# Two transformer mixers: the delta rule's solve is traced ahead of the attention heads, and its products are regrouped

## The chip, the cores and the metric

One core of one Trainium2 chip runs the whole program. The metric is the device time of one execution in microseconds (us). A core has a matrix engine (TensorE: PE in the profile, its weight loads PEld), a vector engine (VectorE, DVE), a scalar engine (ScalarE, ACT), GpSimd (POOL) and a queue engine (SyncE, SP). Each runs its own list of instructions in order; semaphores and DMA landings hold an instruction back until its data are there. TensorE writes its results to PSUM, eight banks of 512 f32 columns per partition, from which VectorE and ScalarE read.

## The reference

The program is two blocks in f32 on 256 tokens of width 1024. The change lies in the second block, whose two layers (l = 0, 1) each hold one mixer and one feed-forward part (dense in layer 0, a mixture of experts in layer 1). The mixer runs two branches on the same normed input h and adds them, gated:

```python
proj = h @ w_in[l]                    # q, k, v of the delta rule; z, b, a; the attention's q, k, v, gates; m_g
qkv = causal_conv_silu(dn_qkv, conv_w[l]);  d_q, d_k, d_v = split(qkv)      # 8 heads of 64
d_q = l2_norm(d_q) * 64 ** -0.5;  d_k = l2_norm(d_k)
o_a = gated_delta_rule(d_q, d_k, d_v, sigmoid(dn_b), g_log)
y_a = (rms_norm(o_a, dn_norm[l]) * silu(dn_z)) @ w_oa[l]
o_b = nsa_core(...)                   # compressed, selected and windowed attention, 8 heads
y_b = o_b @ w_ob[l]
y = (gate_a * y_a + gate_b * y_b) @ w_out[l]
x = x + g_m * y
```

In the delta rule each token t subtracts what earlier tokens left in the state, so the new values X solve a unit lower triangular system per head: (I + L) X = V, with L[t, s] = beta[t] * (k_t . k_s) * exp(g_t - g_s) for s < t. The output is A X, where A holds the same products with q in place of k, kept for s <= t.

## The kernel before

Instructions are traced into a tile framework. Its planner simulates the five engines and, at each moment, gives an engine the ready instruction that was traced first; so the order of the source lines is an order of rank, and work of a lower rank fills the gaps of work of a higher one. What comes out is one fixed list per engine. A tile name with `bufs=n` owns n buffers; a further tile of that name waits until one is released. PSUM is shared as three banks for the linear layers (`pl`), two for the delta rule (`pm`) and three for the attention (`pn`).

Linear layers (`lin_fm`, L263; `lin_tm`, L277) load weights by SP, split each into a high part (`wh`, ScalarE) and a low part (`wl`, VectorE), and multiply in three products (`mm3`, L256). `lin_fm` takes 256 output columns at a time: 48 matmuls for 1024 inputs.

`mixer` (L824) traces in this order: the token-major columns 2048 to 3367 (`lin_tm`, L864, into `tm`); the attention's preparation (`nsa`, L865: compression, norms, rotary embedding, up to `nqT`, `nkT`, `npcT`); q and k of the delta rule with convolution and SiLU (`lin_fm ... conv`, L866, into `dq`); the attention heads (`heads()`, L867: scores, softmax, transposes, into `obh`, `obl`); `delta` (L868); v and z (L869, L870); the rest of the delta rule (`solve()`, L871, into `dz`); then the gates (L886, L887, into `mg`), `w_ob` on the heads' output (`branch_b`, reads `obh`), the split of the solve's output into `oah`, `oal`, and `w_oa` (`branch_a`, reads `oah`). In layer 0 the modulation products (`ada`, tiles `adaw`) fill as well. `w_out` and the feed-forward part read what `branch_a` makes.

`delta` (L900) norms q and k (L905), computes decays, then loops over eight heads (L942): five products into one `pm` bank and an exponential (`ddd`), the key products `p0` (keys of the first 128 tokens against q and k of all 256, 512 columns, L957) and `p_1` (keys of the last 128 against the last 128, 256 columns, L958), each over 64 partitions, two VectorE products into `dUA` (A0, UA1), and the diagonal 16 by 16 blocks, which GpSimd's queue scatters to `dUb`. A 15-step substitution on VectorE inverts these (`dtp`, `dWb`), a round trip through DRAM lays them out (`ds`, `dc16`), and `inv32` widens them to 32 by 32 (`dtf`).

`solve` (L1018) goes through eight row blocks n of 32 tokens, T, cc = n // 4, n % 4. A block subtracts from V the products of L with the X of all blocks before (matmuls `pm<-dX,dUA`), writes `dRt` (VectorE), multiplies by the inverse (`pm<-dRt,dtf`) and copies X out of PSUM (ScalarE, `dX`), each in two halves of four heads. For the second tile (T = 1) every block takes one product with all 128 rows of the first tile's X and, from cc = 1, one with the second tile's:

```python
lst.append((A0(h)[:, 1, 128 + 32 * cc:160 + 32 * cc], X[:, 0, xc]))
if cc:
    lst.append((UA1[0:32 * cc, h, 1, r], X[0:32 * cc, 1, xc]))
```

After blocks 3 and 7 the outputs of a tile are made (`dUA,dX`), normed (`dsq`) and multiplied into `dz`. An f32 product is two matmul instructions in the trace.

Of the kernel before, what the change touches and what calls it, by code (L numbers as in the profile page):

```python
# [26 lines left out]
F32 = mybir.dt.float32  # L27
# [4 lines left out]
AF = mybir.ActivationFunctionType  # L32
OP = mybir.AluOpType
AX = mybir.AxisListType.X
# [55 lines left out]
class Net:  # L90
# [733 lines left out]
    def mixer(self, l):  # L824
        nc, tc, a = self.nc, self.tc, self.a
        with ExitStack() as cx:
            p1 = cx.enter_context(tc.tile_pool(name="m1_%d" % l, bufs=1))
            p2 = cx.enter_context(tc.tile_pool(name="m2_%d" % l, bufs=2))
            p0 = self.p0 = cx.enter_context(tc.tile_pool(name="m0_%d" % l, bufs=1))
            self.tags = dict(rms1=("dsq", 1))  # L830
            ring = p1.tile([128, 4, 2, 256], F32, name="ln", tag="big")
            self.ring = dict(lnt=[ring[:, i] for i in range(2)], lnsq=[ring[:, i] for i in range(2, 4)])
            cw = self.par[l][1]
            mod, scm = self.prep_mod(l, 0, 2, 0)
            hi, lo, X = self.hilo()
            if l == 0:
                self.ada()
                pss = self.nbank()[:, :256]
                add = self.square_sum(p2, pss, True)
                self.apply_ln(p2, 1, then=lambda f, x: add(x))  # L840
                self.rms_stats(pss)
            self.apply_rms(p2, scm, mod[:, 0:8], hi, lo)
            w = a["w_in_2"][l]


            dq = p0.tile([128, 8, 256], F32, name="dq")
            dv = p1.tile([128, 4, 256], F32, name="dv")

            def conv(m0, ps):
                for i in range(2):  # L850
                    m = m0 + i
                    y = p2.tile([128, 256], F32, name="cvy")
                    self.act(y, ps[:, i, :], scale=cw[:, 36 + m:37 + m])
                    for j in range(3):
                        d = 3 - j
                        self.stt(y[:, d:], ps[:, i, :256 - d], cw[:, j * 12 + m:j * 12 + m + 1], y[:, d:],
                                 OP.mult, OP.add)
                    o = dq[:, m, :] if m < 8 else dv[:, m - 8, :]
                    self.sig(o, y)
                    self.tt(o, o, y, OP.mult)  # L860
            tm = p1.tile([128, 2, 1320], F32, name="tm")
            z = p0.tile([128, 4, 256], F32, name="dz")
            self.ring = {}
            self.lin_tm(X, w, 2048, 1320, 8, lambda c, n, T, ps: self.act(tm[:, T, c:c + n], ps), step=440)  # L864
            ob, heads = self.nsa(l, p1, p2, tm)  # L865
            self.lin_fm(X, w, 0, 1024, 8, conv)  # L866
            heads()  # L867
            solve = self.delta(l, p1, p2, dq, dv, tm, z)  # L868
            self.lin_fm(X, w, 1024, 512, 8, lambda m, ps: conv(m + 8, ps))  # L869
            self.lin_fm(X, w, 1536, 512, 8, lambda m, ps: self.silu_ps(z[:, m:m + 2, :], ps))  # L870
            oa = solve()  # L871
            if l == 0:
                self.ada(2)
            mg = [p0.tile([128, 8, 256], F32, name="mg%d" % i, tag=("dq", "mg")[i]) for i in range(2)]

            def gate(i):
                self.lin_fm(X, w, 3368 + i * 1024, 1024, 8, lambda m, ps: self.sig(mg[i][:, m:m + 2, :], ps))

            def branch_b(m, ps):
                g = mg[1][:, m:m + 2, :]  # L880
                self.tt(g, g, ps, OP.mult)

            def branch_a(m, ps):
                g = mg[0][:, m:m + 2, :]
                self.tt(g, g, ps, OP.mult)
                (self.tt if m == 6 else self.ptt)(g, g, mg[1][:, m:m + 2, :], OP.add)  # L886
                self.split(yh[:, m:m + 2, :], yl[:, m:m + 2, :], g)  # L887
            gate(1)
            gate(0)
            if l == 0:  # L890
                self.ada()
            self.lin_fm(ob, a["w_ob_2"][l], 0, 1024, 4, branch_b)
            oah = p0.tile([128, 4, 256], F32R, name="oah", tag="nqT")
            oal = p0.tile([128, 4, 256], F32R, name="oal", tag="nkT")
            self.split(oah, oal, oa)
            yh, yl, Y = self.hilo()
            self.lin_fm(lambda k: (oah[:, k, :], oal[:, k, :]), a["w_oa_2"][l], 0, 1024, 4, branch_a)
        return Y

    def delta(self, l, p1, p2, dq, dv, tm, z):  # L900

        nc, tc, a = self.nc, self.tc, self.a
        c = self.c

        for m in range(0, 8, 2):  # L905
            sq = p2.tile([128, 2, 256], F32, name="dsq", bufs=1)
            self.act(sq, dq[:, m:m + 2, :], AF.Square)
            ps = self.pm.tile([128, 2, 256], F32, name="pm")
# [30 lines left out]
        le = c["le1"][:, :128]  # L939
        A0 = lambda h: UA0[h // 4][:, h % 4]  # L940
        U = lambda h, T: A0(h)[:, 1, 0:128] if T == 0 else UA1[:, h, 1, :]
        for h in range(8):  # L942
            hp, r = h // 2, slice(64 * (h % 2), 64 * (h % 2) + 64)
            gt = p2.tile([128, 2, 128], F32, name="dgt")
            for T in range(2):
                self.ts(gt[:, T, :], c["gt"], g[:, T, h:h + 1], None, OP.mult)
            pe = self.pm.tile([128, 4, 128], F32, name="pm")
            self.mm(pe[:, 0:2, :], gt[:, 0, :], c["le1"].rearrange("p (a b) -> p a b", a=2), True, False, **f)
            self.mm(pe[:, 1, :], g[:, 1, h:h + 1].to_broadcast([128, 128]), le, False, False, **f)
            self.mm(pe[:, 2, :], gt[:, 1, :], le, False, False, **f)  # L950
            self.mm(pe[:, 0, :], self.identb, self.negst, False, False, **f)
            self.mm(pe[:, 2, :], self.identb, self.negst, False, True, **f)
            dd = p2.tile([128, 3, 128], F32, name="ddd")
            self.act(dd, pe[:, 0:3, :], AF.Exp)
            p0 = self.pm.tile([128, 2, 256], F32, name="pm")
            p_1 = self.pm.tile([128, 2, 128], F32, name="pm")
            k = dq[r, 4 + hp, :]  # L957
            self.mm(p0, k[:, 0:128], dq[r, hp::4, :])  # L958
            self.mm(p_1, k[:, 128:256], dq[r, hp::4, 128:256])
            d0 = dd[:, 0:2, :].rearrange("p a b -> p (a b)")  # L960
            self.stt(A0(h), p0, be[:, 0, h:h + 1], d0[:, None, :].to_broadcast([128, 2, 256]), OP.mult, OP.mult)
            self.stt(UA1[:, h], p_1, be[:, 1, h:h + 1], dd[:, 2:3, :].to_broadcast([128, 2, 128]), OP.mult, OP.mult)

            bd = p1.tile([128, 2, 8, 16], F32, name="dbd")
            for T in range(2):
                self.tt(bd[:, T], U(h, T).rearrange("p (b j) -> p b j", j=16), b16, OP.mult)
            nc.vector.tensor_reduce(out=cb[:, :, h], in_=bd.rearrange("p t b j -> p t j b"), op=OP.add, axis=AX)
            for T in range(2):
                q = 64 * T + 8 * h
                nc.gpsimd.dma_start(out=Ub[q:q + 8].rearrange("p s j -> p (s j)"), in_=cb[:, T, h, :])  # L970

        W = p1.tile([128, 2, 16, 16], F32, name="dWb")
        tp = p1.tile([128, 16, 16], F32, name="dtp", tag="dbd")
# [44 lines left out]
    def solve(self, p1, p2, dv, z, A0, UA1, W32, dn, b64, inv32):  # L1018
# [11 lines left out]
        for n in range(8):  # L1030
# [7 lines left out]
                pq = ps[:, :256], ps[:, 256:]  # L1038
            for q in range(2):
                cq = slice(q * 256, q * 256 + 256)  # L1040
                src = V[:, 0, :]
                if n:
                    for h in range(4 * q, 4 * q + 4):
                        xc = slice(h * 64, h * 64 + 64)
                        lst = []
                        if T == 0:
                            lst.append((A0(h)[0:32 * cc, 1, r], X[0:32 * cc, 0, xc]))
                        else:
                            lst.append((A0(h)[:, 1, 128 + 32 * cc:160 + 32 * cc], X[:, 0, xc]))
                            if cc:  # L1050
                                lst.append((UA1[0:32 * cc, h, 1, r], X[0:32 * cc, 1, xc]))
                        for i, (lh, rh) in enumerate(lst):
                            self.mm(pq[q][r, (h % 4) * 64:(h % 4) * 64 + 64], lh, rh, i == 0, i == len(lst) - 1)
                    self.tt(Rt[r, cq], V[r, T, cq], pq[q][r, :], OP.subtract)
                    src = Rt
                for h in range(4 * q, 4 * q + 4):
                    xc = slice(h * 64, h * 64 + 64)
                    self.mm(pq[q][r, (h % 4) * 64:(h % 4) * 64 + 64], W32[r, T * 8 + h, :], src[r, xc])
                self.act(X[r, T, cq], pq[q][r, :])
            if n == 0:  # L1060
                inv32(1)
            if cc == 3:

                sl = slice(T * 128, T * 128 + 128)
# [831 lines left out]
```

## Time and profile before

| what | us |
|---|---|
| median of three runs | 2441.9 (2436.46 to 2446.41) |
| the profiled execution, whole | 2432.33 |
| its span, first to last instruction | 2430.5 |
| PE busy in the span | 2298.8 (95%) |
| DVE busy | 1570.5 (65%) |
| ACT busy | 1282.6 (53%) |
| first mixer: lin_tm's first copy to branch_a's end | about 547 to 828 |
| second mixer: first matmul to branch_a's end | 1114.76 to 1398 |

A busy PE is not a PE at its peak: a matmul of 256 columns lasts 0.28 us in the rows, but the next one starts 0.12 us after it. What PE gets done is read from the starts. PEclk is the granted share of TensorE's clock: 1.00 is 2.4 GHz, 0.5 is 1.2 GHz, and a value between is a stretch with both.

### The profile page before, as it was taken

The numbers are of one execution on the slowest core, as the hardware profiler recorded it, in microseconds if no ns is written. First come the engines' busy times: TensorE is split into PE (matmuls) and PEld (weight loads), VectorE is DVE, ScalarE is ACT, GpSimd is POOL, SyncE is SP. The second block draws the span as 40 slices with busy tenths as digits, with TensorE's granted clock in tenths as the row PEclk, the third lists the DMA queues.
The fourth block names the chain that finished last, engine by engine and source line by source line (L and its number), as shares of the span: only waits on it lengthen the run. The fifth ranks groups of instructions, "written<-read, shape, count | busy, mean of one in ns | idle before, by whom it ended". The sixth has DMA issues, their size and how long they took to land. (4 is left out here: it accounts for less than half of the span.)

```text
span 2430.5 us, 40562 instructions
## 1 busy us (share of the span) xinstructions
PE 2298.8 (95%) x15959; PEld 1870.7 (77%) x15959; DVE 1570.5 (65%) x2353; ACT 1282.6 (53%) x1944; POOL 389.0 (16%) x358
## 2 busy tenths in 40 slices
PE   7999999989999999998999999999999999999987
PEld 7878898878768899997878788888788888644333
DVE  5854777757864576776876469998878888511011
ACT  4654675546645344445756257778777867410010
POOL 2201311220110100000110022322331233000000
PEclk9999999999999999999999899999999999999999
DMA  6454445555354568884323358889898999999998
GB/s 201 142 146 139 159 140 172 169 186 161 115 161 139 169 224 290 282 287 141 120 72 103 133 204 317 335 306 368 315 329 330 348 334 332 370 377 408 408 408 318
DMA packets 275192, 586.92 MB, mean 241 GB/s; under 512 B 30752, under 2 KB 171296, under 8 KB 262704
## 3 DMA queue, kind: packets, MB, share of 16 engines
q1 hardware_dynamic: 260688, 577.28, 66.4%
q0 software_dynamic: 5504, 5.91, 1.4%
q8 instruction: 127, 2.08, 0.4%
q10 hardware_dynamic: 8800, 1.05, 0.3%
q14 instruction: 73, 0.60, 0.1%
HBM read 582.26 MB, written 1.64 MB: 240 GB/s over the span
## 5 line engine op out<-in xcount | busy, mean ns | idle before, releaser
L152 DVE TENSOR_TENSOR wl<-wr,wh 128x1024 fp32r<-128x1024 f32 (+3 forms) x733 | 892.4, 1249 | 307.2 <-ACT wh L149 301.4
L149 ACT ACTIVATE wh<-wr 128x1024 fp32r<-128x1024 f32 (+3 forms) x792 | 773.4, 1006 | 410.7 <-PE pl L172 207.6
L172 PE MATMUL pl<-xTh,wh 128*128 128x256 f32 x1696 | 482.8, 285 | 11.9 <-ACT wh L149 4.9
L172 PE MATMUL pl<-xTh,wl 128*128 128x256 f32 x1696 | 478.9, 284 | 0.9 <-DVE wl L152 0.8
L172 PE MATMUL pl<-xTl,wh 128*128 128x256 f32 x1696 | 478.7, 283 | 0.4 <-DVE xTl L158 0.4
L172 PE MATMUL pl<-wh,eg 128*128 128x448 f32 x1280 | 372.6, 368 | 2.3 <-ACT es L149 2.3
L172 PEld LDWEIGHTS pl<-xTh,wh 128*128 128x128 f32 x1696 | 320.1, 189 | 24.6 <-issue 9.9
L172 PEld LDWEIGHTS pl<-xTl,wh 128*128 128x128 f32 x1696 | 320.3, 189 | 7.8 <-issue 5.7
L172 PEld LDWEIGHTS pl<-xTh,wl 128*128 128x128 f32 x1696 | 319.5, 189 | 8.7 <-issue 6.4
L155 POOL TENSOR_TENSOR wl<-wr,wh 128x896 fp32r<-128x896 f32 (+1 forms) x59 | 189.7, 3216 | 490.4 <-ACT wh L149 386.7
L172 PEld LDWEIGHTS pl<-wh,eg 128*128 128x128 f32 x1280 | 241.7, 189 | 25.1 <-ACT es L149 3.4
L172 PE MATMUL pl<-wl,eg 128*128 128x448 f32 x640 | 238.0, 372 | 14.2 <-POOL wl L155 11.3
L172 PE MATMUL pl<-wr,egf 128*64 128x448 f32 x768 | 163.2, 550 | 5.3 <-DMA wr<-in_w_moe_dram 4.9
L172 PEld LDWEIGHTS pl<-wl,eg 128*128 128x128 f32 x640 | 121.1, 189 | 32.7 <-POOL wl L155 15.1
L172 PEld LDWEIGHTS pl<-wr,egf 128*64 128x64 f32 x768 | 56.2, 137 | 90.0 <-issue 68.6
L172 PE MATMUL pn<-wl,eah 128*128 128x512 f32 x280 | 112.8, 403 | 5.6 <-DVE wl L152 4.1
L172 PE MATMUL pn<-wh,eal 128*128 128x512 f32 x280 | 110.5, 395 | 0.0
L168 DVE TENSOR_SCALAR esu<-pl 128x448 f32<-128x448 f32 x24 | 20.3, 919 | 126.4 <-PE pl L172 126.4
L149 ACT ACTIVATE ehf<-pm 128x448 f32<-128x448 f32 x12 | 6.5, 543 | 165.4 <-PE pn L172 148.6
L172 PE MATMUL pn<-wr,ehf 128*64 128x512 f32 x336 | 86.4, 598 | 5.1 <-DMA wr<-in_w_moe_dram 3.9
L172 PE MATMUL pn<-wh,eah 128*128 128x512 f32 x280 | 89.9, 394 | 0.0
L149 ACT ACTIVATE es<-pl 128x448 f32<-128x448 f32 x64 | 56.9, 989 | 59.6 <-PE pl L172 59.3
(626 smaller groups left out, 3711.8 us busy)
## 6 DMA issues: line engine op xcount, KB each, us to landing
wr<-in_w_moe_dram SPq DMA_DIRECT2D x256, 896.0 KB, 7.1
wr<-in_w_moe_dram SPq DMA_DIRECT2D x96, 1024.0 KB, 8.4
wr<-in_w_dense_dram SPq DMA_DIRECT2D x42, 1024.0 KB, 7.1
wr<-in_w_in_dram SPq DMA_DIRECT2D x32, 1024.0 KB, 5.1
wr<-in_w_in_c_dram SPq DMA_DIRECT2D x30, 1024.0 KB, 5.2
adaw<-in_w_ada_dram SPq DMA_DIRECT2D x48, 512.0 KB, 4.6
adar<-in_w_ada_dram SPq DMA_DIRECT2D x48, 512.0 KB, 5.6
wr<-in_w_in_ab_dram SPq DMA_DIRECT2D x16, 1024.0 KB, 5.2
```

Of the source, the lines that this page charges most:

```text
L149: return self.nc.scalar.activation(out, in_, f, **k)
L152: return self.nc.vector.tensor_tensor(out=out, in0=a, in1=b, op=op)
L155: return self.nc.gpsimd.tensor_tensor(out=out, in0=a, in1=b, op=op)
L168: return self.nc.vector.tensor_scalar(out, a, s1, None, op0=op0)
L172: return self.nc.tensor.matmul(out=out, lhsT=l, rhs=r, start=start, stop=stop, **k)
```

## The change

In `mixer` two calls move: the q and k columns of the delta rule go ahead of `lin_tm`, and `heads()` goes behind `solve()`. In `delta` the loop over eight heads becomes a loop over four pairs: the decays of both heads first, then the two `p0` products back to back (partitions 0 to 63 and 64 to 127), their two VectorE products, the two `p_1` products, theirs, and the diagonal blocks of both. In `solve` the product of the first tile's X with the second tile's rows is taken out of blocks 4 to 7 and made once after block 3, for all 128 rows, and subtracted from V in place.

```diff
             self.ring = {}
+            self.lin_fm(X, w, 0, 1024, 8, conv)
             self.lin_tm(X, w, 2048, 1320, 8, lambda c, n, T, ps: self.act(tm[:, T, c:c + n], ps), step=440)
             ob, heads = self.nsa(l, p1, p2, tm)
-            self.lin_fm(X, w, 0, 1024, 8, conv)
-            heads()
             solve = self.delta(l, p1, p2, dq, dv, tm, z)
...
             oa = solve()
+            heads()
...
-        for h in range(8):
...
-            k = dq[r, 4 + hp, :]
-            self.mm(p0, k[:, 0:128], dq[r, hp::4, :])
-            self.mm(p_1, k[:, 128:256], dq[r, hp::4, 128:256])
...
+        for hp in range(4):
+            dds = []
+            for h in (2 * hp, 2 * hp + 1):
...
+                self.act(dd, pe[:, 0:3, :], AF.Exp)
+                dds.append(dd)
+            rows = [slice(64 * i, 64 * i + 64) for i in range(2)]
+            p0 = [self.pm.tile([128, 2, 256], F32, name="pm") for _ in range(2)]
+            for i, r in enumerate(rows):
+                self.mm(p0[i], dq[r, 4 + hp, 0:128], dq[r, hp::4, :])
...
+            p_1 = [self.pm.tile([128, 2, 128], F32, name="pm") for _ in range(2)]
+            for i, r in enumerate(rows):
+                self.mm(p_1[i], dq[r, 4 + hp, 128:256], dq[r, hp::4, 128:256])
...
-                src = V[:, 0, :]
-                if n:
+                src = V[:, T, :]
+                if cc:
...
+                        u = A0(h)[0:32 * cc, 1, r] if T == 0 else UA1[0:32 * cc, h, 1, r]
+                        self.mm(pq[q][r, (h % 4) * 64:(h % 4) * 64 + 64], u, X[0:32 * cc, T, xc])
...
+            if n == 3:
+                ps = self.pbank()
+                for q in range(2):
+                    cq = slice(q * 256, q * 256 + 256)
+                    for h in range(4 * q, 4 * q + 4):
+                        xc = slice(h * 64, h * 64 + 64)
+                        self.mm(ps[:, xc], A0(h)[:, 1, 128:256], X[:, 0, xc])
+                    self.tt(V[:, 1, cq], V[:, 1, cq], ps[:, cq], OP.subtract)
```

## Rows read from the trace of the kernel before

**Rows 1.** The page, busy time, share of the span and instructions of each engine.

```profile
PE 2298.8 (95%) x15959; PEld 1870.7 (77%) x15959; DVE 1570.5 (65%) x2353; ACT 1282.6 (53%) x1944; POOL 389.0 (16%) x358
```

**Rows 2.** Timeline, PE, solve's burst: start, length, engine, line, op, out<-in, count, [idle].

```profile
1345.71 0.28 PE L172 MATMUL pl<-obh,wh 128*128 128x256 f32 x1
1345.83 0.28 PE L172 MATMUL pl<-obl,wh 128*128 128x256 f32 x1
...
1346.04 1.20 PE L172 MATMUL pm<-dX,dUA 64*32 64x64 f32 x16
1347.16 0.39 PE L172 MATMUL pl<-obh,wl 128*128 128x256 f32 x1
```

**Rows 3.** Timeline, PE, second mixer: the last `branch_b` and the first `branch_a` matmuls.

```profile
1347.63 0.28 PE L172 MATMUL pl<-obh,wl 128*128 128x256 f32 x1
...
1383.65 1.01 PE L172 MATMUL pl<-oah,wh 128*128 128x256 f32 x3 [0.25 <-ACT oah L149]
```

**Rows 4.** Stretches: from:to, length, busy us by engine (x), granted clock, DMA share, GB/s.

```profile
798.55:813.27 14.72, 9.79 (x116) 6.94 (x115) 5.00 (x10) 5.32 (x10) 2.29 (x4) 0.98 0.27 84
813.27:819.53 6.26, 5.99 (x27) 5.70 (x27) 1.22 (x1) 0.00 (x0) 1.31 (x3) 0.51 1.01 308
...
1347.84:1383.65 35.81, 31.17 (x278) 22.25 (x277) 9.34 (x23) 10.10 (x21) 0.41 (x1) 0.75 0.14 45
1383.65:1390.00 6.35, 6.10 (x29) 5.81 (x30) 1.26 (x2) 0.26 (x2) 0.18 (x1) 0.54 1.04 346
...
2150.00:2400.00 250.00, 227.27 (x1168) 99.61 (x1166) 31.71 (x43) 25.16 (x35) 0.00 (x0) 0.99 1.03 409
```

**Rows 5.** Timeline, PE, the same place in the first mixer.

```profile
798.35 0.28 PE L172 MATMUL pl<-obh,wl 128*128 128x256 f32 x1
...
813.29 1.01 PE L172 MATMUL pl<-oah,wh 128*128 128x256 f32 x3 [3.01 <-ACT oah L149]
```

**Rows 6.** Timeline, DVE and ACT, one block of the second mixer's solve.

```profile
1351.61 0.41 DVE L152 TENSOR_TENSOR dRt<-dV,pm 32x256 f32<-32x256 f32 x1 [0.66 <-PE pm L172]
1352.17 0.38 ACT L149 ACTIVATE dX<-pm 32x256 f32<-32x256 f32 x1 [2.43 <-PE pm L172]
```

**Rows 7.** By tile, second mixer, delta rule: ns min/median/max, first and last start.

```profile
L158 DVE SCALAR_TENSOR_TENSOR dUA<-pm,dbe,ddd x16: 478/614/752, 1218.2 to 1277.1; 128x512 f32<-128x512 f32 x8, 128x256 f32<-128x256 f32 x8
...
L152 DVE TENSOR_TENSOR dtp<-dUb,dWb x15: 175/207/225, 1288.9 to 1301.3; 128x15 f32<-128x15 f32 x2, 128x28 f32<-128x28 f32 x2, 128x39 f32<-128x39 f32 x2, 128x48 f32<-128x48 f32 x2
...
L149 ACT ACTIVATE dX<-pm x16: 357/375/377, 1325.9 to 1376.3; 32x256 f32<-32x256 f32 x16
```

**Rows 8.** By tile, second mixer, the heads' softmax and output, and the gates.

```profile
L149 ACT ACTIVATE obh<-pn x4: 384/385/385, 1250.4 to 1321.6; 128x256 fp32r<-128x256 f32 x4
...
L149 ACT ACTIVATE mg<-pl x8: 576/580/595, 1243.6 to 1333.0; 128x512 f32<-128x512 f32 x8
```

**Rows 9.** Lines by form, PE, both mixers' tails: group xcount | busy us, mean ns.

```profile
L172 PE MATMUL pm<-dX,dUA 128*32 128x64 f32 x24 | 3.1, 224 | 0.0
...
L172 PE MATMUL pm<-dX,dUA 128*32 128x64 f32 x64 | 10.4, 278 | 0.9 <-ACT dX L149 0.9
```

**Rows 10.** Timeline, PE, second mixer: key products, and score products of the heads.

```profile
1215.39 1.12 PE L172 MATMUL pm<-dq 64*128 64x512 f32 x2
1216.45 0.39 PE L172 MATMUL pl<-xTl,wh 128*128 128x256 f32 x1
...
1217.12 0.70 PE L172 MATMUL pm<-dq 64*128 64x256 f32 x2
...
1219.67 0.92 PE L172 MATMUL pn<-nkT,nqT 64*128 64x256 f32 x8
...
1229.04 0.92 PE L172 MATMUL pn<-nkT,nqT 64*128 64x256 f32 x4
```

**Rows 11.** By tile, second mixer: the convolution's products and the splits on VectorE.

```profile
L158 DVE SCALAR_TENSOR_TENSOR cvy<-pl,cw1c,cvy x36: 457/476/483, 1161.8 to 1220.0; 128x253 f32<-128x253 f32 x12, 128x254 f32<-128x254 f32 x12, 128x255 f32<-128x255 f32 x12
...
L152 DVE TENSOR_TENSOR wl<-wr,wh x54: 1070/1220/2876, 1110.6 to 1397.7; 128x1024 fp32r<-128x1024 f32 x42, 128x880 fp32r<-128x880 f32 x12
```

More of the change, by code (lines that the diff above doesn't have):

```diff
@@ L941, in delta @@
         U = lambda h, T: A0(h)[:, 1, 0:128] if T == 0 else UA1[:, h, 1, :]
-        for h in range(8):
[L943 to L956, printed above, removed]
-            k = dq[r, 4 + hp, :]
-            self.mm(p0, k[:, 0:128], dq[r, hp::4, :])
-            self.mm(p_1, k[:, 128:256], dq[r, hp::4, 128:256])
[L960 to L970, printed above, removed]
@@ new lines, in delta @@
+        for hp in range(4):
+            dds = []
+            for h in (2 * hp, 2 * hp + 1):
+                gt = p2.tile([128, 2, 128], F32, name="dgt")
+                for T in range(2):
+                    self.ts(gt[:, T, :], c["gt"], g[:, T, h:h + 1], None, OP.mult)
+                pe = self.pm.tile([128, 4, 128], F32, name="pm")
+                self.mm(pe[:, 0:2, :], gt[:, 0, :], c["le1"].rearrange("p (a b) -> p a b", a=2), True, False, **f)
+                self.mm(pe[:, 1, :], g[:, 1, h:h + 1].to_broadcast([128, 128]), le, False, False, **f)
+                self.mm(pe[:, 2, :], gt[:, 1, :], le, False, False, **f)
+                self.mm(pe[:, 0, :], self.identb, self.negst, False, False, **f)
+                self.mm(pe[:, 2, :], self.identb, self.negst, False, True, **f)
+                dd = p2.tile([128, 3, 128], F32, name="ddd")
+                self.act(dd, pe[:, 0:3, :], AF.Exp)
[4 more added lines that the diff above has]
+                self.mm(p0[i], dq[r, 4 + hp, 0:128], dq[r, hp::4, :])
+            for i in range(2):
+                d0 = dds[i][:, 0:2, :].rearrange("p a b -> p (a b)")
+                self.stt(A0(2 * hp + i), p0[i], be[:, 0, 2 * hp + i:2 * hp + i + 1],
+                         d0[:, None, :].to_broadcast([128, 2, 256]), OP.mult, OP.mult)
+            p_1 = [self.pm.tile([128, 2, 128], F32, name="pm") for _ in range(2)]
+            for i, r in enumerate(rows):
+                self.mm(p_1[i], dq[r, 4 + hp, 128:256], dq[r, hp::4, 128:256])
+            for i in range(2):
+                h = 2 * hp + i
+                self.stt(UA1[:, h], p_1[i], be[:, 1, h:h + 1], dds[i][:, 2:3, :].to_broadcast([128, 2, 128]),
+                         OP.mult, OP.mult)
+            for h in (2 * hp, 2 * hp + 1):
+                bd = p1.tile([128, 2, 8, 16], F32, name="dbd")
+                for T in range(2):
+                    self.tt(bd[:, T], U(h, T).rearrange("p (b j) -> p b j", j=16), b16, OP.mult)
+                nc.vector.tensor_reduce(out=cb[:, :, h], in_=bd.rearrange("p t b j -> p t j b"), op=OP.add, axis=AX)
+                for T in range(2):
+                    q = 64 * T + 8 * h
+                    nc.gpsimd.dma_start(out=Ub[q:q + 8].rearrange("p s j -> p (s j)"), in_=cb[:, T, h, :])
@@ L1040, in solve @@
                 cq = slice(q * 256, q * 256 + 256)
-                src = V[:, 0, :]
-                if n:
+                src = V[:, T, :]
+                if cc:
                     for h in range(4 * q, 4 * q + 4):
                         xc = slice(h * 64, h * 64 + 64)
[L1045 to L1053, printed above, removed]
+                        u = A0(h)[0:32 * cc, 1, r] if T == 0 else UA1[0:32 * cc, h, 1, r]
+                        self.mm(pq[q][r, (h % 4) * 64:(h % 4) * 64 + 64], u, X[0:32 * cc, T, xc])
                     self.tt(Rt[r, cq], V[r, T, cq], pq[q][r, :], OP.subtract)
```

## The prediction

> **What bounds the kernel now.** I read the page's busy times first: PE is busy for 95% of the span [rows 1], so work taken off another engine is worth nothing by itself, and the question is where PE does little while it is counted busy. For that I looked, stretch by stretch, at the starts of matmuls against their number. Under the linear layers a matmul of 256 columns starts 0.12 us after the one before, though it lasts 0.28 us [rows 2]. In the second mixer `branch_b`'s last matmul starts at 1347.63 and `branch_a`'s first at 1383.65 [rows 3]. In these 35.81 us the windows show 278 matmuls, all of the solve, at a granted clock of 0.75; the next 6.35 us hold 29 linear matmuls at 0.54 [rows 4]. At 0.118 us each (96 matmuls of `branch_a` in 11.3 us by their starts, at a clock of 1) 29 are 3.4 us of work. The first mixer shows the same more weakly: 798.35 to 813.29 [rows 5], 14.72 us with 116 matmuls, then 27 matmuls in 6.26 us at 0.51 [rows 4]. So the end of each mixer is bound by the solve's chain of dependent steps (PE, VectorE, PE, ScalarE: [rows 6], with 2.43 us of ScalarE's waiting in one block), which nothing covers any more, because all linear work of lower rank has been used up; `branch_a` needs the solve's output, everything after needs `branch_a`.
>
> The chain before that, by tile: the delta rule's eight-head loop holds `dUA` from 1218.2 to 1277.1, the substitution runs from 1288.9 to 1301.3, the solve's `dX` from 1325.9 to 1376.3 [rows 7]. Loop and substitution are ranked behind the heads, whose outputs come at 1250.4 to 1321.6, and the gates `mg`, of a still lower rank, fill from 1243.6 to 1333.0 [rows 8]. So the loop is stretched by the heads to 59 us, and the gates, which could have covered the solve, are used up while both run.
>
> **Tails.** With the solve ahead, heads and gates become the filler and the solve runs inside them. The tail then goes, but its matmuls don't: they must be paid among others. A burst of 16 of them between two linear matmuls pushes the next one from 1345.95 (0.12 after the 1345.83 start) to 1347.16, 1.21 us or 0.076 us each, both switches included [rows 2]. Second mixer: 278 less the 64 of 128 rows (`dX,dUA 128*32`, [rows 9]), which the third part removes, leaves 214, times 0.076 is 16.3 us; the 16 new 128 by 128 by 64 ones I estimate at 0.14 us each (half the 0.278 us that the 128-row ones last in [rows 9]), 2.3 us. 35.8 − 16.3 − 2.3 = 17.2 us. The clock's stretch behind it gives back 6.35 − 3.4 = 2.9 if PE does not go idle-like ahead of `branch_a`. Together 20.1 us. First mixer: 116 − 24 = 92 matmuls remain, 7.0 us, and 14.7 − 7.0 = 7.7; the clock gives 6.26 − 27 × 0.118 = 3.1; the other 40 removed matmuls, which lay under cover, give 40 × 0.076 = 3.0 against 2.3 for the new ones, 0.7. Together 11.5 us. Sum 31.6 us.
>
> **One product for the first tile.** It is counted above in matmuls. On the chain it also takes a burst of 16 (1.2 us) out of three of the four last blocks, 3.6 us, and adds one product of 16 and two VectorE subtractions of 128 by 256 behind block 3, some 2.3 + 0.8 us: about nothing net, and while the solve is no longer last it costs nothing either way.
>
> **Key products.** A `p0` delays the next linear matmul from 1215.39 to 1216.45, 1.06 us, a `p_1` lasts 0.70 [rows 10]. The heads' score products show what a pair on both halves of the array can do: eight matmuls (x8) at 1219.67 last 0.92 us, as four at 1229.04 do [rows 10]. But the pair has to be adjacent in PE's list and both banks free; in the second mixer only one of the eight score pairs stands as such an x8 row. Full pairing would save per mixer 4 × (1.06 + 0.70) = 7.0, so 14 us in both; none saves 0. While one `p0` runs (1.06 us) VectorE can read a 256-column-pair bank in 0.48 to 0.75 us [rows 7], so I take half of the `p0` and no `p_1`: 2.1 us per mixer, 4.2 in all. The Trainium skill (TensorEngine Tiling (Array Packing), Restrictions and Gotchas) says that row tiles of one moment must write to different PSUM banks, which speaks against the pairs in a pool of two; taken at its word, with the exponential's bank often still held, the saving would be 0 and the forecast 4 us later. The trace neither bears it out nor refutes it for `pm`.
>
> What the pair adds is a wait: the second `p0` stands in PE's list behind the first and waits for the other `pm` bank, which the exponential of its decays (or the `p_1` of the pair before) must have left; queued behind it are heads' or linear matmuls. The planner places it when it thinks it ready, so I bound the wait by a VectorE read, 0.5 to 0.75 us, per pair, eight pairs: 0 to 6 us, counted in the range, at 0 in the sum.
>
> **The start of the mixer.** `lin_fm` with convolution now comes first. Of two output groups (256 columns) PE needs 48 × 0.118 = 5.7 us; VectorE six `cvy` of 0.476, two `wl` of 1.22 [rows 11] and about 0.8 of small products: 6.1. In before these lay beside or behind `lin_tm`'s matmuls; now PE may wait for 0.4 us per group on VectorE, four groups, some 2 us per mixer, unless `lin_tm` fills, which it can as soon as its weights are there, behind the conv weights in SP's queue. Bounds: +4 (the delta loop starts earlier than its cover) to −8 us; I take −4. The heads' preparation now gets `tm` one conv later, 23 us.
>
> **Heads late.** They now yield to the delta rule. Their own chain (scores, softmax, transposes) takes some 100 us under mixed load, from the score products at 1219.67 [rows 10] to the last output at 1321.6 [rows 8]. What must follow them is `branch_b` and `branch_a`, 2 × 96 matmuls, 22.7 us. The new end of the mixer is 1398.0 − 20 = 1378 less a little, so the heads are unnoticed if they end by 1353 to 1355, 32 us later than now. The solve needs to be earlier by 18 us only. For half-idle places while the heads wait on softmax and gates have run out I take 2.5 us per mixer, −5 in all; bounds 0 and −20.
>
> **Sum.** 31.6 + 4.2 − 4 − 5 = 26.8, say 27 us. The profiled execution took 2432.3 (its span 2430.5), so 2405; it lies 9.6 below the median of the runs, 2441.9, so for the median 2415. What follows the mixer moves as a block: SP's loads for the feed-forward wait for the mixer's buffers, and from 2150 on DMA is the bound (share 1.03, 409 GB/s, [rows 4]); these loads start as much earlier as the mixer ends, so the gain is kept.
>
> **Rivals.**
>
> A, the heads become the last chain. For it: with conv ahead they start up to 23 us later, and beside a delta loop of higher rank their 100 us grow by a fifth to 120; 1321.6 + 23 + 20 = 1365, 12 us over the deadline. Against it: the loop needs VectorE mainly, and VectorE is at 65% [rows 1]. Price: 12 us per mixer, 24 in all, and 2415 becomes 2439, no change. Chance 0.11.
>
> B, slower: the heads are starved. If the planner gives the loop, the substitution and the solve every free place, and five of the eight rounds of the heads are left when the solve ends near 1330, they need 5 × 100 / 8 = 62 us, then 23 for both branches: 1415, 17 us later than 1398 in the second mixer, and about as much in the first, 34 in all: 2476. It decides from the point at which more than half of the rounds, 4 × 12.5 = 50 us, are left at the solve's end: 1330 + 50 + 23 = 1403. Against it: the substitution and the solve leave PE, ScalarE and most of VectorE free, and fillers of a lower rank did run beside the heads in before (`mg` in [rows 8]). Chance 0.08.
>
> C, the change does not do what it says. The loop needs `dbe` and decays from `tm`, which now comes after conv; heads' preparation (ranked ahead still) may hold VectorE until 1220 as before, so that the loop starts late and the solve moves by less than 10 us. Then the tail stays and only the removed matmuls and pairs count: 4 to 6 us, 2436 to 2438, no change. Chance 0.07.
>
> **How the numbers follow.** Forecast 0.74 at 2415, with its own range from the bounds: the gain is at most 31.6 + 14 + 8, less likely all at once, and 40 to 49 is what I take as its end (2393); at its weak end 31.6 − 8 − 20 − 6 + 4 = 2 us, 2440. The range 2393 to 2441 takes in A and C and leaves B out, and some tails of the forecast. About 0.5%, 12.2 us, is what a measurement of this kernel can tell from no change: faster means below 2429.7. Faster 0.74; same 0.18 (A and C); slower 0.08 (B).
>
> **What would show it.** Right: in the second mixer `branch_b` ends just ahead of `branch_a` with no stretch below a clock of 0.9 between them; the last `dX` comes before 1360 and `dUA` spans less than 45 us; the gates run beside and after the solve; pairs of `pm<-dq` stand as x4 rows of some 1.1 us, at least for half of the `p0`. Wrong: the last wait ahead of `branch_b` is for `obh` from ScalarE with PE at a low clock (A, B); the stretch ahead of the first `oah` matmul is still over 20 us (C); `cvy` spans more than before with PE idle on `pl` (start of the mixer). The single assumption that carries most is that heads and gates suffice as cover for the solve: 214 and 92 matmuls paid at 0.076 us each.

## The result and the profile after

The changed kernel takes 2518.76 us (median of four executions, 2506.51 to 2529.6) where the kernel before takes 2439.18; the ratio is 1.0319, 95% interval 1.0292 to 1.0345. It was forecast 27 us faster and is about 80 us slower, far above the range. The profiled execution took 2523.38, its span 2521.6, 91.1 over the span of before.

The page of the changed kernel, busy times (as [rows 1]):

```profile
PE 2334.5 (93%) x15863; PEld 1898.5 (75%) x15863; DVE 1570.0 (62%) x2353; ACT 1284.5 (51%) x1944; POOL 381.9 (15%) x358
```

PE has 96 matmuls fewer, as the diff says, and is busy 36 us longer: the same work at a lower granted clock, as the stretches below show. By tile, second mixer of the changed kernel, in the form of [rows 7, 8] (ns min/median/max, first and last start):

```profile
L149 ACT ACTIVATE npcT<-pn x1: 574/574/574, 1298.6 to 1298.6; 128x512 f32<-128x512 f32 x1
L149 ACT ACTIVATE nP<-pn,nmn x32: 362/416/479, 1364.1 to 1435.7; 128x128 f32<-128x128 f32 x16, 128x256 f32<-128x256 f32 x16
L149 ACT ACTIVATE obh<-pn x4: 384/386/392, 1391.8 to 1444.2; 128x256 fp32r<-128x256 f32 x4
L149 ACT ACTIVATE mg<-pl x8: 576/579/599, 1285.0 to 1343.5; 128x512 f32<-128x512 f32 x8
L149 ACT ACTIVATE dX<-pm x16: 358/375/377, 1329.6 to 1382.1; 32x256 f32<-32x256 f32 x16
L158 DVE SCALAR_TENSOR_TENSOR dUA<-pm,dbe,ddd x16: 466/614/752, 1213.3 to 1280.6; 128x512 f32<-128x512 f32 x8, 128x256 f32<-128x256 f32 x8
```

The heads' inputs are complete with `npcT` at 1298.6, but their first exponential comes at 1364.1, 65 us later, when the gates (last at 1343.5) have been used up and the solve has 18 us to go. The heads now run alone at the end of the mixer. What they wait for stands on PE just ahead of their first score product, in both mixers (timeline, PE, tiles in `pn`; lines of the first mixer, then of the second):

```profile
753.49 1.12 PE L172 MATMUL pn<-dsq,db 128*128 128x512 f32 x2
754.54 0.70 PE L172 MATMUL pn<-nkT,nqT 64*128 64x256 f32 x2
...
1359.27 2.08 PE L172 MATMUL pn<-dsq,db 128*128 128x512 f32 x2
1361.28 1.65 PE L172 MATMUL pn<-nkT,nqT 64*128 64x256 f32 x4
```

`pn<-dsq,db` is the norm of the solve's first tile, the last product that the solve writes into `pn`. In `solve`, the outputs of the first tile take two of the three `pn` banks (`self.nbank, self.nbank`), those of the second tile two of `pm`. A round of the heads (`scores`) takes two `pn` banks at once. `solve()` is now traced ahead of `heads()`. The banks were not full: after `npcT` (done at 1299.2) the first instruction in the second mixer that touches one is

```profile
1351.90 1.12 PE L172 MATMUL pn<-dUA,dX 128*64 128x128 f32 x8
```

So for 52 us all three stood empty and the heads still did not get them. The reading, which e1, e2 and e5 below test, is that the framework hands out a pool's buffers in the order of the trace: what the heads lack is not space but their turn.

The stretches that answer to [rows 4] (columns as there):

```profile
754.54:843.35 88.81, 78.55 (x543) 53.14 (x543) 38.30 (x121) 36.13 (x106) 2.88 (x6) 0.87 0.19 61
843.35:863.00 19.65, 14.31 (x97) 13.54 (x96) 11.23 (x12) 6.96 (x8) 5.32 (x4) 0.83 0.87 276
1343.50:1361.28 17.78, 15.42 (x99) 11.86 (x99) 3.33 (x6) 5.15 (x11) 0.00 (x0) 0.52 0.10 33
1361.28:1451.60 90.32, 81.22 (x453) 58.34 (x453) 34.94 (x117) 31.46 (x99) 0.00 (x0) 0.70 0.02 6
1451.60:1481.70 30.10, 13.77 (x97) 12.92 (x96) 8.90 (x16) 5.13 (x7) 5.21 (x4) 0.72 1.01 355
```

In the last two stretches ahead of `branch_a` in the second mixer PE does 99 and then 453 matmuls in 108 us, at a granted clock of 0.52 and 0.70. `branch_a` then takes 30.1 us. The reason for that is another wait (timeline of PE, second mixer):

```profile
1460.63 0.28 PE L172 MATMUL pl<-oah,wl 128*128 128x256 f32 x1
1476.69 0.58 PE L172 MATMUL pl<-oah,wh 128*128 128x256 f32 x1 [15.78 <-ACT wh L149]
```

SP's queue in the same stretch (timeline, SP):

```profile
1451.81 5.14 SPq L219 DMA_DIRECT2D wr<-in_w_out_dram  x3
1456.99 5.95 SPq L219 DMA_DIRECT2D wr<-in_w_moe_dram  x3
1463.05 0.65 SPq L219 DMA_DIRECT2D wr<-in_w_oa_dram  x1
```

The last load of `w_oa` stands in SP's list behind three of `w_out` and three of the experts, at a DMA share of 1.01, and PE idles 15.8 us for it. In the kernel before all `w_oa` loads were out by 1346, before the tail.

So the 91.1 us of the span are: the first mixer's first `branch_a` matmul at 843.35 instead of 813.29 [rows 5], 30.1; its `branch_a` slower, 5; the second's at 1451.6 instead of 1383.65 [rows 3], 67.9 less the 35.1 carried over, 32.8; the stall, 15.8; the remaining 7.4 lie behind the mixers.

### The profile page after: what moved, and what is told of

Read it like the earlier page. It is cut to its first block, busy times and chain, and to the rows that moved or that the text cites. A ratio compares the mean times of both kernels' runs of the same rounds, so it can differ in the third digit from the quotient of the medians.

```text
span 2521.6 us, 40372 instructions
## 1 busy us (share of the span) xinstructions
PE 2334.5 (93%) x15863; PEld 1898.5 (75%) x15863; DVE 1570.0 (62%) x2353; ACT 1284.5 (51%) x1944; POOL 381.9 (15%) x358
## 5 line engine op out<-in xcount | busy, mean ns | idle before, releaser
L152 DVE TENSOR_TENSOR wl<-wr,wh 128x1024 fp32r<-128x1024 f32 (+3 forms) x733 | 881.3, 1234 | 352.9 <-ACT wh L149 342.1
L172 PE MATMUL pl<-xTh,wl 128*128 128x256 f32 x1696 | 484.0, 287 | 2.3 <-DVE wl L152 2.3
L172 PE MATMUL pl<-xTl,wh 128*128 128x256 f32 x1696 | 484.0, 286 | 1.9 <-DVE xTl L158 1.9
L172 PEld LDWEIGHTS pl<-xTh,wh 128*128 128x128 f32 x1696 | 326.2, 193 | 31.4 <-ACT xTh L149 10.4
L172 PEld LDWEIGHTS pl<-xTh,wl 128*128 128x128 f32 x1696 | 325.5, 192 | 12.4 <-issue 8.4
L172 PEld LDWEIGHTS pl<-xTl,wh 128*128 128x128 f32 x1696 | 326.2, 192 | 8.7 <-issue 4.4
L172 PE MATMUL pl<-wl,xTh 128*128 128x440 f32 (+2 forms) x208 | 79.3, 381 | 9.4 <-DVE wl L152 9.4
```

Of the source, the lines that this page charges most:

```text
L152: return self.nc.vector.tensor_tensor(out=out, in0=a, in1=b, op=op)
L172: return self.nc.tensor.matmul(out=out, lhsT=l, rhs=r, start=start, stop=stop, **k)
```

## The experiments

Theory P: the heads stand in the order of the `pn` banks behind the solve. Rival R: they lose by rank and by their later preparation.

**e1_bank**: the changed kernel, one line.

```diff
-po, pr = (... for t in ((self.nbank, self.nbank), (self.pbank, self.pbank))[T])
+po, pr = (... for t in ((self.pbank, self.pbank), (self.pbank, self.pbank))[T])
```

> The changed kernel with one edit: the solve's outputs of the first tile take their two PSUM banks from pm, as those of the second tile do, and no longer from pn, the three banks that the heads use. Theory P (the heads stood in the order of the pn banks behind the solve, which is traced first): the first score product comes when npcT is there, near 685 in the first mixer and before 1300 in the second instead of 754.5 and 1361.3; most of the loss goes, 2415 to 2460. Rival R (the heads lose by rank and by their later preparation, no bank is involved): the first score products stay within 10 us of 754 and 1361 and the time stays over 2495.

Measured 2472.52 us, ratio 1.0125 (1.0098 to 1.0152): 46 us go, and 30 stay against the kernel before (2442.27 in that round), so P holds for the larger part only; the time lies above P's range. The first score product comes with `npcT` (by tile, second mixer):

```profile
L149 ACT ACTIVATE npcT<-pn x1: 577/577/577, 1271.1 to 1271.1; 128x512 f32<-128x512 f32 x1
```

and the timeline of PE:

```profile
1270.65 0.92 PE L172 MATMUL pn<-nkT,nqT 64*128 64x256 f32 x8
...
1420.12 0.58 PE L172 MATMUL pl<-oah,wh 128*128 128x256 f32 x1 [14.57 <-ACT wh L149]
```

The stall for `w_oa` is still there, 14.6 us.

**e2_heads_late** and **e5_late_bank**: the kernel before with the heads moved, and the same with the line of e1_bank.

```diff
-            heads()
             solve = self.delta(l, p1, p2, dq, dv, tm, z)
...
             oa = solve()
+            heads()
```

> The kernel before with one edit: heads() is called behind solve(); conv stays behind lin_tm and the attention's preparation, key products and solve stay as they were. Theory P (order of the pn banks): this alone makes the loss, the first score product comes right behind the first tile's norm product (pn<-dsq,db), 2490 to 2530. Rival R2 (the loss is the later preparation, made by conv ahead of lin_tm): the heads are prepared as early as before, so they fill, 2400 to 2445.

> The kernel before with heads() behind solve() and the first tile's outputs of the solve in pm: the change without conv ahead, pairs and the single product, and without the pn order. What is left of the loss in the first of these runs (e1_bank, 30 us) is told apart: if it comes from conv ahead of lin_tm (the attention's preparation 30 to 40 us later), this run gives 2430 to 2450; if it comes from ranking the heads last at all, it stays at 2460 to 2485.

e2 took 2526.47, ratio 1.0348 (1.0293 to 1.0403): moving the heads alone loses as much as the whole change, with `conv` where it was. e5 took 2440.91, ratio 1.0005 (0.9988 to 1.0022): the two banks are the whole loss of this move, 85.6 us, and R falls for it: the heads' rank and their preparation are the same in both. e2's first score product stands behind the norm product, e5's two products behind nothing of the solve (timeline of PE, `pn` tiles, second mixer, of e2):

```profile
1372.03 2.08 PE L172 MATMUL pn<-dsq,db 128*128 128x512 f32 x2
1374.04 1.65 PE L172 MATMUL pn<-nkT,nqT 64*128 64x256 f32 x4
```

and of e5:

```profile
1237.55 0.70 PE L172 MATMUL pn<-nkT,nqT 64*128 64x256 f32 x2
```

But e5 shows as well that the forecast gain does not come when the banks are free. Its tails, from the last `branch_b` to the first `branch_a` matmul (windows, columns as in [rows 4]):

```profile
788.60:817.60 29.00, 24.39 (x205) 17.44 (x203) 6.24 (x12) 6.99 (x14) 2.28 (x4) 0.67 0.19 58
1355.50:1394.70 39.20, 33.70 (x247) 23.65 (x246) 9.70 (x22) 9.39 (x18) 0.58 (x1) 0.62 0.16 52
```

and its X by tile, second mixer:

```profile
L149 ACT ACTIVATE dX<-pm x16: 372/374/377, 1322.5 to 1384.6; 32x256 f32<-32x256 f32 x16
```

29.0 and 39.2 us where before had 14.7 and 35.8; the solve's `dX` spans 62.1 us where it spanned 50.4 [rows 7]. The profiled execution of before lies 9.6 us under its median and that of e5 5.2 over its own, so what is read from the tails is that they did not go, not by how much they grew.

Where the solve loses is seen when its `dX` is split at the end of block 3 into first and second tile. In e5 the first tile has the last round of the heads, the gates and `branch_b` beside it, the second tile nothing more on PE (by tile and windows, second mixer, columns as in [rows 4]):

```profile
L149 ACT ACTIVATE obh<-pn x4: 383/384/385, 1270.7 to 1342.6; 128x256 fp32r<-128x256 f32 x4
1322.50:1356.70 34.20, 33.75 (x421) 28.85 (x409) 16.03 (x31) 17.72 (x35) 0.00 (x0) 1.00 0.29 94
1356.70:1384.60 27.90, 25.21 (x204) 17.53 (x204) 5.92 (x11) 4.90 (x11) 0.00 (x0) 0.65 0.18 57
```

and the first tile of e2, with only the delta rule's own matmuls on PE:

```profile
1349.80:1367.10 17.30, 15.66 (x245) 13.44 (x237) 3.35 (x8) 2.87 (x9) 0.00 (x0) 0.50 0.01 2
```

Covered, the first tile takes 34.2 us at a clock of 1.00; alone, at 0.50, it takes 17.3. In before it took 26.2 (1325.94 to 1352.17), partly covered. `branch_b`, the last of the cover, ends at 1355.4, and the second tile is left over.

**e3_pairs** and **e4_merge**: the kernel before with `delta` alone, and with the single product of `solve` alone, from the change (diffs in the section on the change).

> The kernel before with the key products in head pairs alone. The prediction's step: half of the p0 side by side, 4 us less (0 to 14 less), x4 rows of pm<-dq of some 1.1 us. Rival (the pair's second product waits for the other pm bank): x4 rows are missing or PE waits at pm<-dq, 0 to 6 us more.

> The kernel before with the single product of the first tile's X alone. If the matmuls of the tails are on the chain: the second mixer's stretch from the last branch_b to the first branch_a matmul falls from 35.8 to 27 to 31 us, the first's from 14.7 to 11 to 14, 5 to 12 us less in all. Rival (the chain is latency between PE, VectorE and ScalarE, and the new product with its subtraction adds a link): 0 to 3 us less or more.

e3: 2440.54, ratio 0.9986 (0.9967 to 1.0005), not told from nothing; no two `p0` of a pair stand together; two x4 rows in the first mixer hold the second `p0` and the first `p_1` of a pair (2 + 2, on the two halves). e4: 2442.44, ratio 1.0003 (0.9988 to 1.0018); the tails are 11.8 and 38.5 us, one shorter and one longer. The rival holds for the time: alone it gives nothing. Not for the chain: from the end of block 3 on the solve is shorter in both mixers (32.3 to 27.5 us and 24.1 to 20.9), but its first `dX` comes 4.7 and 7.6 us later (746.8 for 742.1, 1333.5 for 1325.9); why it starts later was not tried.

In the changed kernel the two `p0` of a pair stand apart, for the second waits for the bank of the second head's exponential, and linear matmuls go first (timeline, PE, second mixer):

```profile
1250.78 1.12 PE L172 MATMUL pm<-dq 64*128 64x512 f32 x2
1255.21 1.12 PE L172 MATMUL pm<-dq 64*128 64x512 f32 x2
```

and of ACT:

```profile
1251.95 0.48 ACT L149 ACTIVATE ddd<-pm 128x384 f32<-128x384 f32 x1
```

One x4 row per mixer there, too, is a second `p0` with a first `p_1`; it lasts as long as a `p0` alone (timeline, PE, second mixer):

```profile
1220.89 1.12 PE L172 MATMUL pm<-dq 64*128 64x512 f32 x4
```

**e7_conv_first** and **e9_conv_back**: `conv` ahead of `lin_tm` in the kernel before, and `conv` put back in e1_bank's kernel.

```diff
+            self.lin_fm(X, w, 0, 1024, 8, conv)
             self.lin_tm(X, w, 2048, 1320, 8, ...)
             ob, heads = self.nsa(l, p1, p2, tm)
-            self.lin_fm(X, w, 0, 1024, 8, conv)
```

> The kernel before with the q and k columns ahead of lin_tm alone. The prediction's step: 2 us lost per mixer, bounds 2 gained to 4 lost each: 2438 to 2450. Rival (conv ahead delays the attention's preparation and with it the heads by 20 us or more, which push the solve): 2455 to 2480. Third case (the loop fills the preparation's gaps and ends early): 2410 to 2435.

> The kernel of e1_bank (the changed kernel with the solve's first-tile outputs in pm) with the q and k columns put back behind lin_tm and the attention's preparation. What is left of the loss in e1_bank is 30 us. If conv ahead of lin_tm makes it (heads prepared 46 us later and ranked last), this run is within 0.5% of the kernel before, 2428 to 2445. If it comes from pairs or the single product together with late heads, it stays at 2455 to 2475.

e7: 2450.25, ratio 1.0038 (1.0018 to 1.0058), a small loss just above the end of the first case. e9: 2421.67, ratio 0.9928 (0.9901 to 0.9954), below what was expected: `conv` ahead of `lin_tm` is the second cause, 44 to 51 us beside heads ranked last (against e1; 44 with e13, below), and no stall for `w_oa` is left. Second mixer of e7 by tile:

```profile
L149 ACT ACTIVATE tm<-pl x6: 523/537/537, 1165.2 to 1192.5; 128x440 f32<-128x440 f32 x6
L149 ACT ACTIVATE npcT<-pn x1: 597/597/597, 1267.4 to 1267.4; 128x512 f32<-128x512 f32 x1
L158 DVE SCALAR_TENSOR_TENSOR dUA<-pm,dbe,ddd x16: 466/608/752, 1180.4 to 1251.7; 128x512 f32<-128x512 f32 x8, 128x256 f32<-128x256 f32 x8
```

`tm` ends 41 us later than in before (1151.4) and `npcT` comes 46.6 us later (1220.8 in before), not 23. But 10.5 of these lie ahead of the second mixer, whose first matmul comes at 1125.28 instead of 1114.76 though the first mixer's `branch_a` ends where it did. In the first mixer, which starts as in before, the first copy of `tm` is 28.4 us late, the last 33.9 (602.7 for 568.8) and `npcT` 36.3 (673.5 for 637.2). So the delay by `conv` is some 36 us per mixer. The loop now starts before `tm` is complete (590.5 and 1180.4), since its decays need only the first columns of `tm`; that it makes up the rest behind the first copy is likely, but was not tried.

**e11_bank_oa**: e1_bank with `if l: self.wafter = self.wdma` behind `branch_a`, so that no later weight goes ahead of the last of `w_oa`.

> The kernel of e1_bank, in whose second mixer PE stands 14.6 us in branch_a for the last w_oa weights, queued on SP behind loads of w_out and of the experts; here the loads of w_out and what follows stand behind the last of w_oa in SP's order. If that stall is a price of the late heads: 10 to 15 us less than e1_bank, 2457 to 2463. Rival (the experts' loads come later by as much, so it only moves): 2468 to 2476.

Measured 2451.16, ratio 1.0049 (1.0026 to 1.0072), 21 us under e1_bank, more than expected. The stall in `branch_a` is gone; a shorter one follows, for `w_out` (timeline, PE):

```profile
1410.83 0.58 PE L172 MATMUL pl<-xTh,wh 128*128 128x256 f32 x1 [8.69 <-ACT wh L149]
```

The stalls account for 5.9 of the 21 us. The heads also end earlier (last `obh` at 1380.6 instead of 1387.2); why is not known.

**e6_mid**, **e8_after_mid**, **e10_conv_nsa**, **e12_mid_pairs**: `heads()` between `delta()` and `solve()`, so that the heads take their banks first. In the kernel before (e6); in the changed one (e8); in before with pairs and `conv` between `lin_tm` and `nsa` (e10); in before with pairs (e12).

> The kernel before with heads() between delta() (key products, substitution) and solve(): the loop is ranked ahead of the heads, the solve behind them, so the heads take their pn banks before the solve. If the prediction's tail was right and only the banks' order wrong: dUA spans 40 to 48 us instead of 59, the last dX comes 15 to 25 us earlier, the tail falls from 35.8 to 10 to 20 us, 2410 to 2430. Rival (the heads, pushed back by the loop, become last): the wait ahead of branch_b is for obh, 2440 to 2460.

> The changed kernel with heads() moved back ahead of solve(), behind delta(): conv ahead, pairs and the single product stay. By the order of the pn banks the first score products come right after npcT, as in e1_bank. If the heads' late preparation by conv is the rest of the loss, 2445 to 2475; if their rank behind the solve is, 2410 to 2440.

> A version made from the findings: lin_tm, then q and k with convolution, then the attention's preparation, delta with paired key products, heads, v and z, solve. The loop should start 15 to 25 us earlier than in before without delaying tm; the heads take their pn banks ahead of the solve. If the delta rule's path is the bound: 2405 to 2425. Rival (the preparation and so the heads come 20 us or more later and become last, as with conv ahead of lin_tm): 2435 to 2455.

> The kernel of e6_mid (heads between delta and solve) with the key products in head pairs. Pairs alone measured 0.9986 of the kernel before (2 to 3 us). If the pairs shorten the loop, which is now on the path: 2 to 8 us less than e6_mid, 2421 to 2427. Rival (the loop is bound by VectorE, not by its matmuls): within 2 us of e6_mid, 2427 to 2431.

e6: 2428.66, ratio 0.995 (0.9934 to 0.9967), 10 us faster; `dUA` spans 52.8 us instead of 59, the last `dX` comes at 1371.1 instead of 1376.3, so both less than expected, and the second tail is still 29.8 us (1348.7 to 1378.5): the time is in the range, the signs are not. e8: 2462.35, ratio 1.008 (1.0055 to 1.0105): with `conv` ahead 20 us of loss stay though the heads are not behind the solve. e12: 2436.24, 0.9981 (0.9962 to 0.9999): neither case, with the pairs it is 7.6 us slower than e6. e10: 2448.01, 1.0026 (1.001 to 1.0042), the rival's case: against e12, from which it differs by that alone, `conv` ahead of the preparation costs 12 us even behind `lin_tm`.

**e13_conv_back2** to **e16_mid_all**: e9's kernel in more executions; e5 with the single product (e14); e5 with the pairs (e15); e6 with pairs, single product and `pm` (e16).

> The kernel of e9_conv_back once more, in more executions: 2421.7 was the median of five that lay at 2420.6 to 2425.5 and, the profiled one, at 2444.4. If the gain is real: 2419 to 2426. If the four were a chance: 2432 to 2445.

> The kernel before with heads() behind solve(), the first tile's outputs in pm, and the single product for the first tile. If the single product pays once the solve runs beside the heads (64 matmuls less per mixer, each paid among others at 0.076 us: 2 x 4.9 us less, 2 x 2.3 more): 5 us under e5_late_bank, 2432 to 2438. If it makes the whole of e9_conv_back's gain: 2418 to 2428. If nothing: 2438 to 2444.

> The kernel before with heads() behind solve(), the first tile's outputs in pm, and the key products in pairs. If the pairs pay as in the kernel before (3 us): 2435 to 2440. If they make the whole of e9_conv_back's gain: 2418 to 2428.

> The kernel of e6_mid (heads between delta and solve) with pairs, the single product and the first tile's outputs in pm. If e6_mid's 10 us and what the parts give beside it add up: 2415 to 2425. Rival (the single product and pm, which has two banks only, lengthen the solve's chain, which here ends last): 2428 to 2440.

e13: 2428.24, ratio 0.9952 (0.993 to 0.9973), between its two cases: e9's gain is real but smaller. e14: 2425.39, ratio 0.9933 (0.9915 to 0.9952), its second case. e15: 2445.44, ratio 1.0012 (0.9991 to 1.0034), above both its cases, so pairs give nothing beside late heads. e16: 2433.4, ratio 0.9967 (0.9949 to 0.9985), the rival's case. The single product, worth nothing alone, is worth 15.5 us beside late heads (2440.91 to 2425.39), and 17.2 with pairs added to both (e15 to e13); in e16, with the heads ahead of the solve, it and the banks in `pm` are worth 2.8 (from e12). e14's tails (windows), to be read against e5's:

```profile
793.40:812.50 19.10, 13.70 (x124) 11.30 (x124) 5.83 (x12) 5.30 (x11) 2.29 (x5) 0.66 0.21 64
1349.20:1376.50 27.30, 23.37 (x191) 19.48 (x190) 9.33 (x21) 9.06 (x18) 0.58 (x1) 0.68 0.24 75
```

and its X by tile:

```profile
L149 ACT ACTIVATE dX<-pm x16: 373/374/377, 1313.6 to 1366.2; 32x256 f32<-32x256 f32 x16
```

The first tile is as long as in e5 (35.3 us for 34.2, first mixer 35.1 for 34.7). The gain is in the second tile: 17.3 us for 27.9, first mixer 28.0 for 34.3, together 16.9. Two steps of it, on PE the matmuls of `dX,dUA` and `dRt,dtf` twice, of e5 and then of e14 (windows):

```profile
1365.90:1379.30 13.40, 13.40 (x98) 8.79 (x96) 1.68 (x4) 1.50 (x4) 0.00 (x0) 0.50 0.01 1
1358.70:1366.10 7.40, 7.40 (x66) 6.68 (x64) 1.69 (x4) 1.50 (x4) 0.00 (x0) 0.50 0.00 0
```

PE counts as busy throughout both, at the same clock of 0.50 and with nothing of the heads left: here the solve's own matmuls are the chain, and 32 fewer of them take 6.0 us less.

e14, the heads behind the solve, the first tile's outputs in `pm`, and the single product, is the version to keep: faster than both kernels, with `conv` and the key products as they were.

## Why the prediction was wrong

**The step that failed** is "with the solve ahead, heads and gates become the filler". It took the order of the trace for a rank on engines alone. It is also the order in which PSUM banks are handed out: the solve's first tile stood ahead of the heads for two of the three, and the heads waited until its turn had come, with the banks empty. The two calls of `nbank` stood in `solve`, and the prediction never asked which pools the moved work shares. e2 against e5, one line apart, shows the size: 85.6 us.

**Rival B** had the sign and the place (heads left over at the solve's end) but the wrong mechanism and price: it starved them by rank, with five of eight rounds left, 34 us in all. All eight were left when the solve's first tile was done: the first score product came at 1361.28, and they ended at 1444.2, 83 us later. Its argument against itself, that fillers of lower rank run while the substitution leaves engines free, was true of engines and did not matter.

**Tails** was the largest term, 31.6 us. It priced the solve's matmuls among others at 0.076 us each and let the tail go. With the banks free (e5) the tails are 29.0 and 39.2 us, not zero, and this is a second step that failed: the cover lengthens the chain. Laid beside gates and `branch_b` the first tile takes 34.2 us instead of the 17.3 that it takes alone, and in the second mixer gates and `branch_b` are used up before the second tile begins. From the first `dUA` to the last `dX` the path takes 158.8 us in e5, with the loop ranked ahead of the heads, and took 158.1 in before [rows 7]. That the loop is "stretched by the heads to 59 us" holds in small part only: ranked ahead of them it takes 54.6 (1225.8 to 1280.4 in e5) and 52.8 (e6). The best version gains 16 us.

**One product** was forecast at "about nothing net" on the chain: 3.6 us out of the last blocks against 3.1 for the new product. Measured in the second tile it takes out 10.6 and 6.3 us, the new product included (e14 against e5), and the first tile grows by less than 1.2. Mis-sized was the price of a burst: 1.2 us for 16 matmuls is that of a stretch at a clock of 1, and the last blocks run alone at 0.50, where PE is what they wait for. Alone the product also shortens the second tile, but the solve starts later by as much or more (e4).

**Key products** were forecast at half of the `p0` side by side, 4.2 us. In the changed kernel no two `p0` are: 4.4 us lie between those shown, for the two `pm` banks are the exponentials' as well. The measured 0.14% (e3) is inside its interval of nothing, and beside e6 the pairs cost 7.6 us. The Trainium skill (TensorEngine Tiling (Array Packing), Restrictions and Gotchas) says that row tiles must write to different PSUM banks. The x4 row at 1220.89 agrees, its four matmuls filling the two `pm` banks in the 1.12 us of two; no run has a pair in one bank. Taken at its word, the prediction said, it would make the saving 0, and 0 is what came, for the banks were taken.

**The start** was forecast at 4 us lost for both mixers, with bounds of 4 gained and 8 lost, and the heads' inputs at 23 us late. Alone it costs 0.38%, some 9 us, and `npcT` comes some 36 us late in either mixer (e7). Mis-sized was this delay. Beside heads ranked last it costs 44 to 51 us (e1 against e13 and e9), part of it the stall.

**The shift as a block** was nearly right: 7.4 of the 91.1 us are from behind the mixers. But it passed over SP's order inside the mixer's end: with `branch_a` late, loads of `w_out` and of the experts stood ahead of the last of `w_oa`.

Of the signs named, "the last wait ahead of `branch_b` is for `obh` with PE at a low clock" was the one that came, with 0.70 over 90 us; of the signs of being right, `branch_b` did end just ahead of `branch_a`, but because both stood behind the heads.

## What to carry to other kernels

Before work is ranked ahead of other work, list the rotating buffers that both take, PSUM first: the work behind gets its buffer only after all that is traced ahead of it, whatever the engines do and however empty the buffers are. A dependent chain is not hidden at the price of its instructions: beside other work each link waits (34.2 us instead of 17.3 here), so ask first how long the chain becomes and whether the cover lasts to its end. What was left over of it ran at a clock of 0.50 here, with PE busy throughout, so taking matmuls out of it paid (e14). After such a move read the queue engine's list at the stage's end: a weight load that had slipped behind the next stage's loads kept the matrix engine waiting for 15.8 us here.

## What was not expected of the hardware

One load of 512 KB that was issued behind six large ones held PE for 15.8 us at a DMA share of 1.01 and 355 GB/s (14.6 in e1). With its place given back (e11) the program was 21 us faster, though 8.7 us of waiting came back one stage later; the stall less these is 5.9, so most of the 21 has another cause, which stays open.

The chain of the solve's first tile was twice as fast alone at a granted clock of 0.50 (17.3 us, e2) as among linear matmuls at 1.00 (34.2 us, e5).
